# Up stage issued in written order, ten groups computed ahead, fewer score steps a load

## Chip, cores, metric

The kernel runs on one core of a Trainium2 chip. The metric is the device time of one execution in microseconds (us); smaller is better. All data are float32. A product is made from two parts of each operand, a rounded high part and the rest (hi and lo), as three matmuls: hi by hi, hi by lo, lo by hi.

## Reference, cut to what matters

One layer of a decoder on 1024 tokens of width 1024:

```
h = rmsnorm(x);  z = h @ w_in                      # seven blocks of 512 columns
mix_a = gated linear recurrence of four blocks     # chunks, decays, states
mix_b = gate_b * causal_conv3(gate_c * conv_h)
x = x + rmsnorm(concat(mix_a, mix_b) @ w_out)
h = rmsnorm(x);  u = causal_conv3(h @ ffn_w_up)    # 1024 -> 2 x 2816
gate, val = split(u)
x = x + rmsnorm((silu(gate) * val) @ ffn_w_down)   # 2816 -> 1024
```

## The kernel before, in words

The instructions are written in Python; a list scheduler then orders each engine's instructions by its own cost model, with the place in the program as priority. Each engine runs its list in order. `high_priority` lifts what stands in it.

**Mixers.** The 1024 tokens are two halves of 512. For each half come projections of 512 columns (f, q, i, g: `gemm_quad`, eight k tiles of 128 rows, loaded and split two at a time) and twelve convolution tiles (`gemm_tile`, three for each of four column blocks, in `z_conv`). Small steps of the recurrence wait in a queue, `fill`. `tick` pops one between blocks of matmuls. The score steps come first: products and diagonals, then fourteen "levels" (seven widths by two groups of heads). A level is eight short matmuls `sl` (L358), then on DVE a predicated copy (L359) and three multiplications (L364, L366, L368), on whose result the next level's matmuls wait. Chunk steps follow. `rate` says how many ticks a load of two k tiles gets (L206). `z_conv` pops a number per tile from `rates`.

**Front.** The first weights of f come in two halves (`pieces=2`, L130), cast on DVE (L132, L133). x comes transposed, tile by tile (L229); ACT scales its hi part (L232), DVE makes its lo part (L233). A small chain (L594 to L599) makes the bound of the forget gate.

**Up stage.** The product by `w_up` and its convolution run in 22 groups (`order`: gate column block j and so on), each a 2x2 Strassen-Winograd scheme with seven products, P1 to P7, of 12 matmuls of 512 columns. A group has two PSUM banks `pG` (g) and two `pV` (v):

- `head_weights` loads the group's 1 MB of weights w (L729) and splits two of the four blocks (h_x, l_x). `head_1` is P1 into g[1], copied to g[0] by ACT (L753); `head_2` is P2 onto g[0].
- `mid_weights` makes three sums on DVE (L774 to L776) and splits them into h_t (ACT) and l_t (DVE). These tiles exist once, so group n's h_t can only be written when P7 of group n-1 has read the old ones.
- `mid` is P6 onto g[1], a copy s2 of it by ACT (L741), P5 into v[1], v[0] = v[1] + s2 on DVE (L791), P7 onto g[1], a copy s3, and v[1] += s3 on DVE (L794).
- `tail_weights` splits the last two blocks (h_b, l_b). P4 (onto g[1]) and P3 (onto v[0]) use them, in the next group's turn of the loop.
- `gate` is a convolution of g (ACT L803, DVE L804, L805) and a Silu (L817). `value` is the same of v, then the product with the gate (L824) and, after each second group, four sums for the down stage (L832 to L835).

In the trace the weights' names tell the products: c2 is P6, c1 P5, c7 P7, c4 P4, c3 P3, uhi and ulo P1 and P2.

**Groups ahead.** P1 and P2 need only the first token half. For the groups in `AHEAD` they are computed before the loop, in pairs (`ahead`, matmuls `pA`), between the output projection and the loop, and stored; `take_back` loads them and ACT copies them into g (L768). Such a group is "short": in the loop it has P3 and P4 of the group before and its own P6, P5, P7. A long group has P1, P4, P2, P3, P6, P5, P7. `AHEAD` holds eight groups: 0, 1, 3, 5, 7, 9, 11, 13. `marked` (L737) is a matmul that only sets a bank's state. While the `pA` run, ACT and DVE build the right operands of P3 to P7 (comb, L858 to L879).

The down stage follows: seven products, with 44 k tiles of gated values read back.

Of the kernel before, what the change touches and what calls it, by code (L numbers as in the profile page):

```python
# [2 lines left out]

# [1 line left out]

# [36 lines left out]
def decoder_kernel(ctx: ExitStack, tc: tile.TileContext, x, xT, w_sq, w_cv, w_out, w_up, w_dn,  # L42
# [68 lines left out]
    def split(src, hi, lo):  # L111
        nc.scalar.copy(hi, src)  # L112
        nc.vector.tensor_tensor(lo, src, hi.bitcast(F32), ALU.subtract)  # L113

    def load_w(src, shape, name, pieces=1, queue=None, gains=None):

        raw = wp.tile(list(shape), F32, tag="wraw", bufs=3, name=f"r_{name}")
        hi = wp.tile(list(shape), F32R, tag="whi", name=f"h_{name}")
        lo = wp.tile(list(shape), F32R, tag="wlo", name=f"l_{name}")
        if gains is not None:  # L120
            nc.sync.dma_start(raw[:], src)
            for i, g in enumerate(gains):
                nc.scalar.mul(hi[:, i], raw[:, i], g)
                nc.vector.scalar_tensor_tensor(
                    lo[:, i], raw[:, i], g, hi[:, i].bitcast(F32), ALU.mult, ALU.subtract)
            return hi, lo
        n = shape[1] // pieces
        for i in range(pieces):
            s = slice(i * n, (i + 1) * n)
            (queue or nc.sync).dma_start(raw[:, s], src[:, s])  # L130
            if queue is not None:
                nc.vector.tensor_copy(hi[:, s], raw[:, s])  # L132
                nc.vector.tensor_tensor(lo[:, s], raw[:, s], hi[:, s].bitcast(F32), ALU.subtract)  # L133
            else:
                split(raw[:, s], hi[:, s], lo[:, s])
        return hi, lo
# [28 lines left out]
    def mm3_fm(ps, whi, wlo, ahi, alo, first, last, more=False):  # L165
        nc.tensor.matmul(ps, whi, ahi, start=first, stop=False, skip_group_check=more)  # L166
        nc.tensor.matmul(ps, whi, alo, start=False, stop=False, skip_group_check=more)  # L167
        nc.tensor.matmul(ps, wlo, ahi, start=False, stop=last, skip_group_check=more)  # L168

    def mm3_tm(ps, ahi, alo, whi, wlo, first, last, more=False):  # L170
        nc.tensor.matmul(ps, ahi, whi, start=first, stop=False, skip_group_check=more)  # L171
        nc.tensor.matmul(ps, ahi, wlo, start=False, stop=False, skip_group_check=more)  # L172
        nc.tensor.matmul(ps, alo, whi, start=False, stop=last, skip_group_check=more)  # L173

    def gemm_tile(src, act, name):

# [6 lines left out]
    def gemm_quad(src, act, name, token_major, groups, order=None, pieces=1, rate=1, hooks=None, queue=None,  # L183
                  gains=None, banks=None):

        order = order or list(range(len(act)))
        pss = [banks(f"p_{name}_{j}") if banks else ps_mm.tile([P, TH], F32, tag="mm", name=f"p_{name}_{j}")
               for j in range(4)]
        ws, i0 = {}, 0
        for gi, n in enumerate(groups):  # L190
            ks = range(i0, i0 + n)
            for i in ks:
                if i // 2 not in ws:
                    ws[i // 2] = load_w(src[order[i] // 2], (P, 2, TH), f"{name}_{i // 2}", pieces,
                                         queue if i == 0 else None, (gains or {}).get(order[i] // 2))
            for j in range(4):
                for i in ks:
                    whi, wlo = (w[:, i % 2, :] for w in ws[i // 2])
                    js = slice(j * P, (j + 1) * P)
                    ahi, alo = act[order[i]]  # L200
                    first, last = i == 0, i == len(act) - 1
                    if token_major:
                        mm3_tm(pss[j][:], ahi[:, js], alo[:, js], whi, wlo, first, last)
                    else:
                        mm3_fm(pss[j][:], whi[:, js], wlo[:, js], ahi, alo, first, last)
                if (i0 + n) % 2 == 0 and j % (4 // rate) == 4 // rate - 1:  # L206
                    tick()
            i0 += n
            if hooks and gi in hooks:
                hooks[gi]()  # L210
        return pss
# [13 lines left out]
    def make_h(hf):  # L225
        act = []
        for k in range(KD):
# [2 lines left out]
            hi, lo = hslot(f"hi{hf}_{k}"), hslot(f"lo{hf}_{k}")  # L230
            g = vcol(V_PRE + k)
            nc.scalar.mul(hi[:], xk[:], g)  # L232
            nc.vector.scalar_tensor_tensor(lo[:], xk[:], g, hi[:].bitcast(F32), ALU.mult, ALU.subtract)  # L233
            act.append((hi[:], lo[:]))
            if hf == 0:
                yield act
# [337 lines left out]


    hgen = make_h(0)
    act_a = next(hgen)

    class Lazy:


        def __len__(self):
            return KD

        def __getitem__(self, k):
            while len(act_a) <= k:
                next(hgen)
            return act_a[k]


    lbt = zp.tile([P, 4, H], F32, name="lbt")
    lbp = vec[:, V_LB : V_LB + H]
    e_, s_, lb, oml = (lbt[:, i, :] for i in range(4))
    nc.vector.tensor_tensor(e_, lbp, lbp, ALU.subtract)  # L594
    nc.scalar.activation(e_, e_, AF.Exp)
    nc.vector.reciprocal(s_, e_)
    nc.vector.tensor_tensor(s_, s_, e_, ALU.mult)
    nc.vector.tensor_tensor(lb, s_, s_, ALU.subtract)
    nc.vector.tensor_scalar(oml, lb, -1.0, 1.0, ALU.mult, ALU.add)  # L599

    first = {}

    def scale_a():
        for _ in hgen:
            pass
        nc.sync.dma_start(ident[:], ident_d)
        with tc.high_priority():
            pc = aux("pc", (P, NC_H + P))
            for c in range(NC_H):
                nc.tensor.matmul(pc[:, c : c + 1], sums[0][:, c * C : (c + 1) * C], ones[:, 0:1], start=True, stop=True)  # L610
            first["r"] = rstd(pc[:, :NC_H], D, "x0")
            first["rows"] = by_token(0, first["r"], pc[:NC_H, NC_H:])

    def scale_a_rows():
        nc.scalar.activation(warm[:], first["r"][:, 0:1], AF.Sigmoid)
        first["FU"] = evac_f(0, pss, first["rows"])

    pss = gemm_quad(w_sq[0], Lazy(), "f0", False, (1, 1, 1, 1, 1, 1, 1, 1), pieces=2, queue=nc.sync,
                    hooks={6: scale_a})
    r0 = first["r"]  # L620
    qss = gemm_quad(w_sq[1], act_a, "q0", False, PAIRS, hooks={0: scale_a_rows}, banks=aux)
# [12 lines left out]
    def mixers(hf, act, F, UW, rb, rq, r, ma, conv_rates, at_end=None):  # L634
        fill.extend(score_steps(hf, F, UW))
        v = evac_v(hf, gemm_quad(w_sq[2], act, f"i{hf}", True, PAIRS, rate=2), rq)
        gg = evac_g(hf, gemm_quad(w_sq[3], act, f"g{hf}", True, PAIRS, rate=2), r)
        fill.extend(chunk_steps(hf, F, UW, v, gg, ma))
        mb = z_conv(hf, act, rb, conv_rates, at_end)
        return [(ma[0][:, j, :], ma[1][:, j, :]) for j in range(H)] + mb  # L640
# [1 line left out]
    def ma_tiles(hf):  # L642
# [1 line left out]

    act_b = []
    later = []
    mix_a = mixers(0, act_a, F0, UW0, rb0, rq0, r0, ma_tiles(0), (1, 1, 1, 1, 1, 1, 1, 1, 1, 1, 2, 2),
                   at_end=(lambda: later.append(stats(1)), lambda: act_b.extend(list(make_h(1))[-1])))
    r1 = later[0]

# [7 lines left out]
    gain = post_gain(0, ap)  # L658
    x1a = out_proj(0, mix_a, gain)
    evac_q(1, gemm_quad(w_sq[1], act_b, "q1", False, PAIRS, rate=2), rb1, UW1)  # L660
    mix_b = mixers(1, act_b, F1, UW1, rb1, rq1, r1, ma_tiles(1), (1, 1, 1, 1, 1, 1, 1, 1, 2, 2, 2, 2))
    a1 = []
    x1b = out_proj(1, mix_b, gain, hooks={0: lambda: make_a1(x1a, a1), 1: lambda: tick(len(fill))})

# [11 lines left out]
    take(1, [a1[k][0] for k in range(KH)], [a1[k][1] for k in range(KH)])  # L676
    take(2, [a1[k + KH][0] for k in range(KH)], [a1[k + KH][1] for k in range(KH)])

    def product(ps, w, i, op, first=False):
        hi, lo = w  # L680
        for k in range(KH):
            mm3_fm(ps, hi[:, i, k], lo[:, i, k], a_hi[op][k], a_lo[op][k], first and k == 0, k == KH - 1, not first)

    order = [j + s * NG for j in range(NG) for s in range(2)]
    box = [{} for _ in order]
    AHEAD = (0, 1, 3, 5, 7, 9, 11, 13)
    nc.vector.tensor_scalar(neg[:], vec[:, V_PREF : V_PREF + KH], -1.0, None, ALU.mult)


    ah_w = zh.tile([P, 2, 2, KH, P], F32, tag="F", name="ah_w")
# [3 lines left out]
    def ahead(ns, keep):  # L696
# [4 lines left out]
        to = [keep.get(n, ah_f[:, i]) for i, n in enumerate(ns)]  # L701
        for p, op in ((1, 1), (0, 2)):
            for i, n in enumerate(ns):
                product(banks[i][:], (ah_x[:, i, 0], ah_x[:, i, 1]), p, op, p == 1)
                nc.scalar.copy(to[i][:, p], banks[i][:])
                if p == 0 and n not in keep:
                    nc.sync.dma_start(f_d[n], to[i])

    for i in (1, 3, 5):
        ahead(AHEAD[i : i + 2], {})  # L710
    tick(len(fill))
    scope1.close()
# [5 lines left out]
    def ft(tag, shape, name, bufs=1, dt=F32, pool=None):  # L718
        return (pool or fp).tile(list(shape), dt, tag=tag, bufs=bufs, name=name)

    def parts(src, tags, shape, name, bufs=1, pool=None):
        hi = ft(tags[0], shape, f"h{name}", bufs, F32R, pool)
        lo = ft(tags[1], shape, f"l{name}", bufs, F32R, pool)
        split(src, hi[:], lo[:])
        return hi, lo

    def load_up(n):
# [7 lines left out]
    def marked(ps):  # L735

        nc.tensor.matmul(ps, a_hi[1][0][:, :P], a_hi[1][0], start=True, stop=True)  # L737

    def snap(ps, name):
        t = ft("s", (P, TH), name, 4, pool=pa[0])  # L740
        nc.scalar.copy(t[:], ps)  # L741
        return t

    def head_weights(n):
        b = box[n]
        w = b["w"] = load_up(n)
        b["x"] = parts(w[:, 0:2], ("xh", "xl"), (P, 2, KH, P), f"_x{n}", 2, pb[0])

    def head_1(n):
        b = box[n]  # L750
# [8 lines left out]
    def take_back(n):  # L759
# [5 lines left out]
        if n < 2:  # L765
            marked(g[:, 0])
            marked(g[:, 1])
        nc.scalar.copy(g[:], t[:])  # L768

    def mid_weights(n):  # L770
        b = box[n]
# [7 lines left out]
    def mid(n):  # L779
# [8 lines left out]
            product(v[:, 1], b["t"], 1, 5, True)  # L788
        if n < 2:
            marked(v[:, 0])  # L790
        nc.vector.tensor_tensor(v[:, 0], v[:, 1], s2[:], ALU.add)  # L791
        product(a, b["t"], 2, 7)
        s3 = snap(a, f"s3_{n}")
        nc.vector.tensor_tensor(v[:, 1], v[:, 1], s3[:], ALU.add)  # L794

    def tail_weights(n):
        b = box[n]
# [20 lines left out]

    def value(n):
        b = box[n]  # L820
        v = ft("av", (P, T), f"v{n}", 2, pool=pa[0])
        conv(b.pop("v"), v, NF + order[n])
        g = b["o"]
# [325 lines left out]
```

## Time and profile before

| | us |
|---|---|
| median of 3 runs | 1128.95 |
| the profiled execution | 1128.56 |
| its span (first to last instruction) | 1126.7 |
| busy: PE, weight loads, DVE, ACT | 1103.9, 910.6, 839.1, 511.2 |

| stretch, us | stage |
|---|---|
| 0 to 430 | mixers of both halves, first output projection |
| 430 to 517 | second output projection, groups ahead |
| 517 to 907 | up stage |
| 907 to 1127 | down stage, last rows |

PE is the matmul engine, PEld its weight load, DVE the vector engine, ACT the scalar engine, SP the engine that issues most DMAs. Matmuls are pipelined: one of 512 columns is shown as 0.39 us long, but the next starts 0.227 us after it. So time is lost where starts lie further apart. A row of the timeline gives start, length, engine, line, operation, output and inputs, count, and in brackets the idle time before and what ended it.

### The profile page before, as it was taken

What the parts mean: (1) busy time and instruction counts of PE and PEld (TensorE: products, weight loads), DVE (VectorE), ACT (ScalarE), POOL (GpSimd) and SP (SyncE); (2) the same over time, 40 slices, a digit from 0 to 9 for tenths busy, and PEclk for the clock granted to TensorE, in tenths of its full rate; (3) what the DMA queues carried; (4) which work ended last, traced back from release to release, by engine and by line L of the source; (5) the groups of instructions that cost most, each with busy time, mean ns of one, the idle gap of its engine ahead of it and who ended that gap; (6) DMA issues with size and microseconds to landing.
All of it is one profiled execution on the core that took longest, in us unless ns stands there. A gap on an engine that the chain in (4) does not pass through costs nothing.

```text
span 1126.7 us, 13472 instructions
## 1 busy us (share of the span) xinstructions
PE 1103.9 (98%) x5090; PEld 910.6 (81%) x5090; DVE 839.1 (74%) x1199; ACT 511.2 (45%) x755; POOL 10.0 (1%) x18
## 2 busy tenths in 40 slices
PE   9999999999999999999999999999999999999997
PEld 7878888888878888877787777878888888888885
DVE  7578677537687777387989888887878866865787
ACT  6444254435433337366443544444444534445541
POOL 1100000000000000000000000000000000000000
PEclk9999999999999999999999999999999999999999
DMA  8522224325312237174323434233222369867633
GB/s 289 208 65 71 94 77 132 119 94 187 113 57 94 83 109 259 64 253 169 112 103 140 159 122 154 76 126 140 103 85 93 122 215 410 336 225 251 200 109 121
DMA packets 55088, 167.23 MB, mean 148 GB/s; under 512 B 5480, under 2 KB 5744, under 8 KB 52080
## 3 DMA queue, kind: packets, MB, share of 16 engines
q1 hardware_dynamic: 54704, 165.76, 42.1%
q8 instruction: 40, 0.66, 0.3%
q0 software_dynamic: 160, 0.52, 0.1%
q14 instruction: 24, 0.20, 0.1%
q10 hardware_dynamic: 160, 0.09, 0.0%
HBM read 132.01 MB, written 34.34 MB: 148 GB/s over the span
## 4 chain that ended last, share of the span: by engine, by line
PE 88%; DVE 5%; ACT 4%; DMA 2%; issue 1%; DVEq 0%; SPq 0%; ACTq 0%
PE pG L166 7%; PE pG L167 7%; PE pG L168 7%; PE pV L166 3%; PE pV L168 3%; PE pV L167 3%; PE pX L171 3%; PE pX L173 3%; PE pX L172 3%; PE pY L171 2%; PE pY L172 2%; PE pY L173 2%; PE sl L358 2%; PE p_wo L173 2%; PE p_wo L171 2%; PE p_wo L172 2%
## 5 line engine op out<-in xcount | busy, mean ns | idle before, releaser
L113 DVE TENSOR_TENSOR ls<-s,hs 128x1024 fp32r<-128x1024 f32 (+1 forms) x40 | 45.2, 1129 | 44.9 <-ACT hs L112 44.9
L112 ACT CAST hs<-s 128x1024 fp32r<-128x1024 f32 (+1 forms) x40 | 39.1, 977 | 73.4 <-PE pY L172 31.2
L172 PE MATMUL pY<-lw,hs 128*128 128x512 f32 x132 | 51.3, 389 | 0.0
L173 PE MATMUL pY<-hw,ls 128*128 128x512 f32 x132 | 51.3, 389 | 0.0
L171 PE MATMUL pY<-hw,hs 128*128 128x512 f32 x132 | 51.2, 389 | 0.0
L817 ACT ACTIVATE g<-g 128x1024 f32<-128x1024 f32 x22 | 23.4, 1062 | 59.2 <-DVE g L805 59.2
L112 ACT CAST h_t<-t 128x1536 fp32r<-128x1536 f32 x22 | 32.6, 1481 | 38.5 <-PE pG L167 35.8
L113 DVE TENSOR_TENSOR l_t<-t,h_t 128x1536 fp32r<-128x1536 f32 x22 | 38.6, 1756 | 9.6 <-ACT h_t L112 9.6
L171 PE MATMUL pX<-hw,hs 128*128 128x512 f32 x116 | 45.1, 389 | 0.0
L172 PE MATMUL pX<-lw,hs 128*128 128x512 f32 x116 | 45.1, 389 | 0.0
L173 PE MATMUL pX<-hw,ls 128*128 128x512 f32 x116 | 45.1, 389 | 0.0
L166 PE MATMUL pG<-uhi,h_x 128*128 128x512 f32 x112 | 44.4, 396 | 0.0
L167 PE MATMUL pG<-ulo,h_x 128*128 128x512 f32 x112 | 44.3, 395 | 0.0
L168 PE MATMUL pG<-uhi,l_x 128*128 128x512 f32 x112 | 44.1, 394 | 0.0
L166 PE MATMUL pG<-c2h,h_t 128*128 128x512 f32 x88 | 34.9, 396 | 8.0 <-ACT h_t L112 6.7
L804 DVE SCALAR_TENSOR_TENSOR v<-pV,vec,v 128x1023 f32<-128x1023 f32 x22 | 28.2, 1280 | 18.0 <-ACT v L803 17.9
L113 DVE TENSOR_TENSOR l_b<-w,h_b 128x1024 fp32r<-128x1024 f32 x22 | 26.8, 1220 | 17.3 <-ACT h_b L112 17.3
L803 ACT ACTIVATE g<-pG,vec 128x1024 f32<-128x1024 f32 x22 | 24.5, 1115 | 28.7 <-PE pG L168 28.6
L803 ACT ACTIVATE v<-pV,vec 128x1024 f32<-128x1024 f32 x22 | 24.5, 1112 | 26.6 <-PE pV L168 26.5
L359 DVE COPY_PREDICATED S<-m_lev,sl 128x512 f32<-128x512 uint8 x28 | 24.9, 891 | 14.8 <-PE sl L358 14.8
L345 ACT COPY lhs<-UW 128x512 f32<-128x512 f32 x28 | 18.5, 662 | 37.3 <-DVE UW L366 37.3
L166 PE MATMUL pG<-c4h,h_b 128*128 128x512 f32 x88 | 34.8, 395 | 0.7 <-ACT s L741 0.7
(339 smaller groups left out, 3416.5 us busy)
## 6 DMA issues: line engine op xcount, KB each, us to landing
w<-w_up SPq DMA_DIRECT2D x22, 1024.0 KB, 4.8
b<-w_dn SPq DMA_DIRECT2D x35, 512.0 KB, 8.6
s<-s_d SPq DMA_DIRECT2D x33, 512.0 KB, 4.7
s_d<-g SPq DMA_DIRECT2D x22, 512.0 KB, 3.3
s_d<-S SPq DMA_DIRECT2D x11, 768.0 KB, 3.9
r_wo<-w_out SPq DMA_DIRECT2D x16, 512.0 KB, 3.5
xT<-xT SPq DMA_DIRECT2D x16, 256.0 KB, 3.8
r_q<-w_sq SPq DMA_DIRECT2D x8, 512.0 KB, 3.8
```

The source lines that it names most:

```text
L112: nc.scalar.copy(hi, src)
L113: nc.vector.tensor_tensor(lo, src, hi.bitcast(F32), ALU.subtract)
L166: nc.tensor.matmul(ps, whi, ahi, start=first, stop=False, skip_group_check=more)
L167: nc.tensor.matmul(ps, whi, alo, start=False, stop=False, skip_group_check=more)
L168: nc.tensor.matmul(ps, wlo, ahi, start=False, stop=last, skip_group_check=more)
L171: nc.tensor.matmul(ps, ahi, whi, start=first, stop=False, skip_group_check=more)
L172: nc.tensor.matmul(ps, ahi, wlo, start=False, stop=False, skip_group_check=more)
L173: nc.tensor.matmul(ps, alo, whi, start=False, stop=last, skip_group_check=more)
L359: nc.vector.copy_predicated(view(S, 2 * X, o + h, (X - h, 2), (2 * h, n), (1, h)), m_lev[:, li].rearrange("p x g (b h) -> p x (g b) h", h= ...
L803: nc.scalar.mul(a[:], c, wc[2])
L804: nc.vector.scalar_tensor_tensor(a[:, 1:], c[:, : T - 1], wc[1], a[:, 1:], ALU.mult, ALU.add)
L817: nc.scalar.activation(g[:], g[:], AF.Silu)
```

## The change

- `product` puts an edge from the last product to the next (`issue_after`), so the loop's products go out on PE as written; those of `ahead` are free.
- In `value`, v[1] += s3 now stands behind P3; v[0] = v[1] + s2 gets high priority.
- `AHEAD` has ten groups at even places: 0, 2, ..., 18.
- ACT's split of h_x is issued behind the s3 copy two groups before; ACT's copy in `take_back` is kept in program order.
- The g projection has (2, 1, 2, 1) ticks a load in place of 2 each; the convolution tiles get two more, spread over the list.
- In the front, the first weights are issued ahead of x, their second half by ACT; DVE's lo part of x is issued behind the first weight cast; the chain of the gate's bound moves to the end of the first projection.

```diff
-            (queue or nc.sync).dma_start(raw[:, s], src[:, s])
+            (queue[i] if queue else nc.sync).dma_start(raw[:, s], src[:, s])
             if queue is not None:
-                nc.vector.tensor_copy(hi[:, s], raw[:, s])
+                front.append(nc.vector.tensor_copy(hi[:, s], raw[:, s]))
...
+                r = rate[i0 // 2] if isinstance(rate, tuple) else rate
+                if (i0 + n) % 2 == 0 and j % (4 // r) == 4 // r - 1:
                     tick()
...
-            nc.vector.scalar_tensor_tensor(lo[:], xk[:], g, hi[:].bitcast(F32), ALU.mult, ALU.subtract)
+            with tc.issue_after(front[0].ins):
+                nc.vector.scalar_tensor_tensor(lo[:], xk[:], g, hi[:].bitcast(F32), ALU.mult, ALU.subtract)
...
-    nc.vector.tensor_tensor(e_, lbp, lbp, ALU.subtract)
+    def lower_bound():
+        tc.keep_in_program_order(nc.vector.tensor_tensor(e_, lbp, lbp, ALU.subtract))
...
         nc.sync.dma_start(ident[:], ident_d)
+        lower_bound()
...
-        gg = evac_g(hf, gemm_quad(w_sq[3], act, f"g{hf}", True, PAIRS, rate=2), r)
+        gg = evac_g(hf, gemm_quad(w_sq[3], act, f"g{hf}", True, PAIRS, rate=(2, 1, 2, 1)), r)
...
-    mix_a = mixers(0, act_a, F0, UW0, rb0, rq0, r0, ma_tiles(0), (1, 1, 1, 1, 1, 1, 1, 1, 1, 1, 2, 2),
+    mix_a = mixers(0, act_a, F0, UW0, rb0, rq0, r0, ma_tiles(0), (2, 1, 1, 2, 1, 1, 2, 1, 1, 2, 1, 1),
...
-    mix_b = mixers(1, act_b, F1, UW1, rb1, rq1, r1, ma_tiles(1), (1, 1, 1, 1, 1, 1, 1, 1, 2, 2, 2, 2))
+    mix_b = mixers(1, act_b, F1, UW1, rb1, rq1, r1, ma_tiles(1), (2, 1, 2, 1, 2, 1, 2, 1, 2, 1, 2, 1))
...
+    line = []
-    def product(ps, w, i, op, first=False):
+    def product(ps, w, i, op, first=False, in_line=True):
         hi, lo = w
-        for k in range(KH):
-            mm3_fm(ps, hi[:, i, k], lo[:, i, k], a_hi[op][k], a_lo[op][k], first and k == 0, k == KH - 1, not first)
+        with tc.issue_after(line[-1]) if in_line and line else nullcontext():
+            for k in range(KH):
+                mm = mm3_fm(ps, hi[:, i, k], lo[:, i, k], a_hi[op][k], a_lo[op][k], first and k == 0, k == KH - 1,
+                            not first)
+        if in_line:
+            line.append(mm.ins)
...
-    AHEAD = (0, 1, 3, 5, 7, 9, 11, 13)
+    AHEAD = (0, 2, 4, 6, 8, 10, 12, 14, 16, 18)
...
-    for i in (1, 3, 5):
+    for i in range(1, len(AHEAD) - 1, 2):
         ahead(AHEAD[i : i + 2], {})
...
-        b["x"] = parts(w[:, 0:2], ("xh", "xl"), (P, 2, KH, P), f"_x{n}", 2, pb[0])
+        b["x"] = parts(w[:, 0:2], ("xh", "xl"), (P, 2, KH, P), f"_x{n}", 2, pb[0], snaps[2 * n - 3] if n > 1 else None)
...
-        nc.scalar.copy(g[:], t[:])
+        tc.keep_in_program_order(nc.scalar.copy(g[:], t[:]))
...
-        nc.vector.tensor_tensor(v[:, 0], v[:, 1], s2[:], ALU.add)
+        with tc.high_priority():
+            nc.vector.tensor_tensor(v[:, 0], v[:, 1], s2[:], ALU.add)
         product(a, b["t"], 2, 7)
-        s3 = snap(a, f"s3_{n}")
-        nc.vector.tensor_tensor(v[:, 1], v[:, 1], s3[:], ALU.add)
+        b["s3"] = snap(a, f"s3_{n}")
...
     def value(n):
         b = box[n]
+        c22 = b["v"][:, 1]
+        nc.vector.tensor_tensor(c22, c22, b.pop("s3")[:], ALU.add)
```

## Rows read from the trace of the kernel before

**Rows 1.** The page: busy time by engine, share of the span, instructions.

```profile
PE 1103.9 (98%) x5090; PEld 910.6 (81%) x5090; DVE 839.1 (74%) x1199; ACT 511.2 (45%) x755; POOL 10.0 (1%) x18
```

**Rows 2.** PE's waits over the span: total us, times, longest us.

```profile
PE pG L166 <- ACT h_t L112: 6.7, 5, 1.3
PE sl L358 <- DVE UW L366: 2.8, 7, 0.5
...
PE pG L166 <- DVE S L835: 1.3, 1, 1.3
PE pG L166 <- ACT s L741: 0.7, 1, 0.7
```

**Rows 3.** Windows: us, PE, PEld, DVE, ACT, POOL busy (count), clock, DMA, GB/s.

```profile
666.34:700.85 34.51, 33.18 (x144) 26.97 (x144) 29.56 (x31) 16.73 (x19) 0.00 (x0) 1.00 0.36 134
...
806.92:845.46 38.54, 38.54 (x170) 31.57 (x169) 30.71 (x31) 16.80 (x20) 0.00 (x0) 1.00 0.28 102
...
468.66:517.48 48.82, 48.62 (x225) 39.21 (x224) 42.45 (x75) 34.56 (x64) 0.00 (x0) 1.00 0.56 203
```

**Rows 4.** Timeline of PE where short group 9 begins.

```profile
664.62 0.39 PE L168 MATMUL pG<-c7h,l_t 128*128 128x512 f32 x1
666.34 0.50 PE L166 MATMUL pG<-c2h,h_t 128*128 128x512 f32 x1 [1.34 <-DVE S L835]
...
667.14 0.40 PE L166 MATMUL pG<-c4h,h_b 128*128 128x512 f32 x1
```

**Rows 5.** Timelines of ACT and DVE around the same place.

```profile
656.15 1.01 ACT L768 COPY pG<-f 128x1024 f32<-128x1024 f32 x1
...
664.82 1.47 ACT L112 CAST h_t<-t 128x1536 fp32r<-128x1536 f32 x1 [4.62 <-PE pG L167]
666.19 0.58 ACT L741 COPY s<-pG 128x512 f32<-128x512 f32 x1
...
663.01 0.69 DVE L791 TENSOR_TENSOR pV<-pV,s 128x512 f32<-128x512 f32 x1
...
666.32 1.76 DVE L113 TENSOR_TENSOR l_t<-t,h_t 128x1536 fp32r<-128x1536 f32 x1
...
673.28 1.28 DVE L804 SCALAR_TENSOR_TENSOR v<-pV,vec,v 128x1023 f32<-128x1023 f32 x1 [0.88 <-ACT v L803]
```

**Rows 6.** Start of the up stage: PE, SP's weight loads, and their landing (page).

```profile
527.00 0.39 PE L168 MATMUL pG<-c7h,l_t 128*128 128x512 f32 x1
528.07 0.50 PE L166 MATMUL pG<-c4h,h_b 128*128 128x512 f32 x1 [0.68 <-ACT s L741]
...
521.39 1.37 SPq L729 DMA_DIRECT2D w<-w_up  x2
...
w<-w_up SPq DMA_DIRECT2D x22, 1024.0 KB, 4.8
```

**Rows 7.** Score levels of the second half: PE and DVE; one of the first half.

```profile
318.34 1.14 PE L358 MATMUL sl<-UW,lhs 128*128 128x128 f32 x8 [0.44 <-DVE UW L366]
...
317.50 0.69 DVE L366 TENSOR_TENSOR UW<-UW,F 128x512 f32<-128x512 f32 x1
...
116.78 0.73 DVE L359 COPY_PREDICATED S<-m_lev,sl 128x512 f32<-128x512 uint8 x1
```

**Rows 8.** Timeline of the front: SP, ACT, DVE and PE.

```profile
0.73 0.39 SPq L229 DMA_DIRECT2D xT<-xT  x1
1.19 0.89 SPq L130 DMA_DIRECT2D r_f<-w_sq  x2
...
4.78 0.71 ACT L232 ACTIVATE hi<-xT,vec 128x512 fp32r<-128x512 f32 x1
...
5.60 0.75 DVE L233 SCALAR_TENSOR_TENSOR lo<-xT,vec,hi 128x512 fp32r<-128x512 f32 x1
6.27 0.76 DVE L132 CAST h_f<-r_f 128x512 fp32r<-128x512 f32 x2
...
6.83 0.47 PE L166 MATMUL p_f<-hi,h_f 128*128 128x512 f32 x1 [1.57 <-DVE h_f L132]
```

More of the change, by code (lines that the diff above doesn't have):

```diff
@@ L1 @@
 from collections import deque
-from contextlib import ExitStack
+from contextlib import ExitStack, nullcontext
 import numpy as np
@@ L113, in split @@
         nc.vector.tensor_tensor(lo, src, hi.bitcast(F32), ALU.subtract)
+    front = []
     def load_w(src, shape, name, pieces=1, queue=None, gains=None):
@@ L167, in mm3_fm @@
         nc.tensor.matmul(ps, whi, alo, start=False, stop=False, skip_group_check=more)
-        nc.tensor.matmul(ps, wlo, ahi, start=False, stop=last, skip_group_check=more)
+        return nc.tensor.matmul(ps, wlo, ahi, start=False, stop=last, skip_group_check=more)
     def mm3_tm(ps, ahi, alo, whi, wlo, first, last, more=False):
@@ L172, in mm3_tm @@
         nc.tensor.matmul(ps, ahi, wlo, start=False, stop=False, skip_group_check=more)
-        nc.tensor.matmul(ps, alo, whi, start=False, stop=last, skip_group_check=more)
+        return nc.tensor.matmul(ps, alo, whi, start=False, stop=last, skip_group_check=more)
     def gemm_tile(src, act, name):
@@ L205, in gemm_quad @@
                         mm3_fm(pss[j][:], whi[:, js], wlo[:, js], ahi, alo, first, last)
-                if (i0 + n) % 2 == 0 and j % (4 // rate) == 4 // rate - 1:
+                r = rate[i0 // 2] if isinstance(rate, tuple) else rate
+                if (i0 + n) % 2 == 0 and j % (4 // r) == 4 // r - 1:
                     tick()
@@ L576, in decoder_kernel @@
     hgen = make_h(0)
-    act_a = next(hgen)
     class Lazy:
+        made = ()
         def __len__(self):
@@ L585, in __getitem__ @@
         def __getitem__(self, k):
-            while len(act_a) <= k:
-                next(hgen)
-            return act_a[k]
+            while len(self.made) <= k:
+                self.made = next(hgen)
+            return self.made[k]
     lbt = zp.tile([P, 4, H], F32, name="lbt")
@@ L593, in decoder_kernel @@
     e_, s_, lb, oml = (lbt[:, i, :] for i in range(4))
-    nc.vector.tensor_tensor(e_, lbp, lbp, ALU.subtract)
[L595 to L599, printed above, removed]
+    def lower_bound():
+        tc.keep_in_program_order(nc.vector.tensor_tensor(e_, lbp, lbp, ALU.subtract))
+        nc.scalar.activation(e_, e_, AF.Exp)
+        nc.vector.reciprocal(s_, e_)
+        nc.vector.tensor_tensor(s_, s_, e_, ALU.mult)
+        nc.vector.tensor_tensor(lb, s_, s_, ALU.subtract)
+        nc.vector.tensor_scalar(oml, lb, -1.0, 1.0, ALU.mult, ALU.add)
     first = {}
@@ L616, in scale_a_rows @@
         first["FU"] = evac_f(0, pss, first["rows"])
-    pss = gemm_quad(w_sq[0], Lazy(), "f0", False, (1, 1, 1, 1, 1, 1, 1, 1), pieces=2, queue=nc.sync,
+    act_a = Lazy()
+    pss = gemm_quad(w_sq[0], act_a, "f0", False, (1, 1, 1, 1, 1, 1, 1, 1), pieces=2, queue=(nc.sync, nc.scalar),
                     hooks={6: scale_a})
@@ L677, in decoder_kernel @@
     take(2, [a1[k + KH][0] for k in range(KH)], [a1[k + KH][1] for k in range(KH)])
-    def product(ps, w, i, op, first=False):
+    line = []
+    def product(ps, w, i, op, first=False, in_line=True):
         hi, lo = w
-        for k in range(KH):
-            mm3_fm(ps, hi[:, i, k], lo[:, i, k], a_hi[op][k], a_lo[op][k], first and k == 0, k == KH - 1, not first)
+        with tc.issue_after(line[-1]) if in_line and line else nullcontext():
[4 more added lines that the diff above has]
+            line.append(mm.ins)
     order = [j + s * NG for j in range(NG) for s in range(2)]
     box = [{} for _ in order]
-    AHEAD = (0, 1, 3, 5, 7, 9, 11, 13)
-    nc.vector.tensor_scalar(neg[:], vec[:, V_PREF : V_PREF + KH], -1.0, None, ALU.mult)
+    AHEAD = (0, 2, 4, 6, 8, 10, 12, 14, 16, 18)
+    tc.keep_in_program_order(
+        nc.vector.tensor_scalar(neg[:], vec[:, V_PREF : V_PREF + KH], -1.0, None, ALU.mult))
     ah_w = zh.tile([P, 2, 2, KH, P], F32, tag="F", name="ah_w")
@@ L703, in ahead @@
             for i, n in enumerate(ns):
-                product(banks[i][:], (ah_x[:, i, 0], ah_x[:, i, 1]), p, op, p == 1)
+                product(banks[i][:], (ah_x[:, i, 0], ah_x[:, i, 1]), p, op, p == 1, False)
                 nc.scalar.copy(to[i][:, p], banks[i][:])
@@ L719, in ft, with parts @@
         return (pool or fp).tile(list(shape), dt, tag=tag, bufs=bufs, name=name)
-    def parts(src, tags, shape, name, bufs=1, pool=None):
+    def parts(src, tags, shape, name, bufs=1, pool=None, behind=None):
         hi = ft(tags[0], shape, f"h{name}", bufs, F32R, pool)
         lo = ft(tags[1], shape, f"l{name}", bufs, F32R, pool)
-        split(src, hi[:], lo[:])
+        with tc.issue_after(behind) if behind else nullcontext():
+            nc.scalar.copy(hi[:], src)
+        nc.vector.tensor_tensor(lo[:], src, hi[:].bitcast(F32), ALU.subtract)
         return hi, lo
@@ L737, in marked @@
         nc.tensor.matmul(ps, a_hi[1][0][:, :P], a_hi[1][0], start=True, stop=True)
+    snaps = []
     def snap(ps, name):
         t = ft("s", (P, TH), name, 4, pool=pa[0])
-        nc.scalar.copy(t[:], ps)
+        snaps.append(nc.scalar.copy(t[:], ps).ins)
         return t
```

## The prediction

> **What bounds the kernel now.** First the page's busy times: PE is busy 98% of the span [rows 1], which leaves at most 22.8 us for any change that takes no matmul away. The list of PE's waits is next: the largest by far is PE waiting for ACT's h_t in the up stage, 6.7 us in 5 waits, and a sixth of the same length is put down to DVE's L835 [rows 2]; after it come 2.8 us in 7 waits of the score levels. Third, the windows by pair of groups. A pair of long groups takes 38.54 us with PE busy throughout, 2.75 us for each of its 14 products. A pair of one long and one short group has 12 products, 33.0 us at that pace, and takes 34.51 [rows 3]. Last the timeline at a short group's start: P7 of the group before ends, two matmuls of P6 come next and wait 1.34 us, and P4, whose operands were long there, stands behind them [rows 4]. ACT begins h_t at 664.82, within P7's last matmul, because the tile exists once; PE goes on as it ends [rows 5]. The place in the order costs the time, not the amount of ACT's or DVE's work: ACT had idled 4.62 us before that cast.
>
> **The change part by part.**
>
> *Written order.* In a short group P3 and P4 now come before P6: 24 matmuls, 5.5 us, in which h_t (1.47) and l_t (1.76) can be made [rows 5]. One wait costs 1.72 us between starts less 0.227, and 0.11 more for the first matmul after it (0.50 in place of 0.39) [rows 4]: 1.60 us. Six of them: -9.6 us. What is late next is the s3 copy of 0.58, which P4 needs and P3 covers with 2.75 us, and v[0] = v[1] + s2, which P3 needs: DVE started it at 663.01 and took 0.69 [rows 5], so it was done 1.3 us before P7 ended, and it now has priority.
>
> *Group 1 becomes long.* At 528.07 P4 of group 0 waited for s3: 1.07 us between starts less 0.227, plus 0.11: 0.95 us [rows 6]. P1 of group 1 now lies between them: -0.95. P1 needs its 1 MB of weights, issued at 521.39 and 4.8 us on the way [rows 6], then h_x and l_x, some 2.3 us by the nearest casts (h_t and l_t, of half as many columns again, take 3.2 [rows 5]): 528.5, a microsecond too late as things stand. But the start of the loop moves back by a whole pair ahead, 10.9 us of PE, with at most 5 us more for ACT (four copies of 0.58 and two casts shorter than 1.47 [rows 5]), so the load goes out earlier; I take 0, with +1.2 as the other end. Two marking matmuls fall away, 0.45 us, but they filled PE's wait for s2 before P7 of group 0: together 0.
>
> *Two more groups ahead.* Their P1 and P2 move from the loop to the stretch before it, PE's time unchanged. That stretch is dense now: 48.62 of 48.82 us [rows 3]. One more boundary between pairs, at the price of the three there are (0.2 us idle together): 0 to 0.4, I take +0.2. The added DMAs (half a megabyte of weights, a store and a load for each group) find queues busy 0.56 before the loop and 0.36 in it [rows 3]; without that cover they would delay a copy that is needed some 5 us after its group's turn begins. SP carries them in line with the weight loads.
>
> *The s3 addition behind P3.* The same 0.69 us of DVE, now ahead of ACT's value pass; off PE's path as long as the two v banks suffice. 0.
>
> *Ten short groups instead of six that mattered.* Each pair must fit 29.56 us of DVE into 33.0 [rows 3], 90%, where the long pairs run at 80% without a wait. The cost of that is what the trace does not show: nothing at one end; at the other 1.5 us a pair, which would be today's 34.5. The short windows today wait for order and not for DVE, so I take the value near the lower end, 0.1 us a pair: +1.0.
>
> *Front.* PE starts at 6.83, when DVE's weight cast is done; the cast began at 6.27, behind the lo part of x (0.75 from 5.60) [rows 8]. With the weights issued 0.46 earlier and cast first, PE can start when ACT's hi part is there: 4.78 + 0.71, and the x transfer one issue slot (0.46) later: about 6.0. Its second matmul then needs the lo part, 0.75 more. So 0.5 gained, between 0 and 0.9. The chain of the gate's bound is about a microsecond of tiny instructions on DVE, hidden beside the q projection, and would cost that microsecond if it were not. One page speaks against more from ACT's queue: the Trainium skill, DMA: Bandwidth & Descriptors, section "Issuing engines are not separate DMA queues", says that all issuing engines share the same transfer engines and only issue time is saved. By it the sum stays; with a stream of its own for the second half it would be 0.4 us less. No row here tells the two apart.
>
> *Score steps.* A wait costs its idle time plus the 0.16 between a matmul's modelled end and the next start: 0.60 at 318.34 [rows 7]. In the second half three levels of the g projection wait; with four ticks at 24 matmuls' distance instead of 12, two of these should go, and one that did not wait may start to. -0.7, between -1.1 and 0. In the first half the waits are in the first ticks, which keep their places: 0. The two displaced steps meet the convolution tiles.
>
> **The sum.** 1128.56 - 9.6 - 0.95 + 0.2 + 1.0 - 0.5 - 0.7 = 1118.0 for the profiled execution; the median stands 0.4 above it, so 1118.4 for the median, 0.9% less. A difference under about 0.5% can't be told from none here.
>
> **Rivals.**
>
> *ACT's order keeps P6 waiting.* The copy from `take_back` (1.01) is kept in program order, which puts it behind s3 and ahead of h_t: 0.58 + 1.01 + 1.47 + 1.76 = 4.8 us after P7 [rows 5], some 5.2 with handovers, against 5.5 and 0.45 until l_t is first read. If DVE begins a value pass (1.28) or the s3 addition (0.69) just before l_t, that is 6.5 to 7.2, and P6 waits 0.5 to 1.2 us in ten groups: 1123.5 to 1130, I say 1125. The Trainium skill, TensorE: Matmul & The Clock Gate, section "Architectural detail", calls the queues of ACT and DVE strictly first in, first out; by that rule such a wait is not mended at run time. The trace agrees: at 656.15 the copy stood between two passes [rows 5] and nothing overtook it. For it: the slack is only 0.7 us. Against: the scheduler knows of l_t's reader. Chance 0.15.
>
> *DVE becomes the bound (slower).* Today's long and short pair leaves DVE 4.95 us idle (34.51 - 29.56), mostly until ACT passes arrive. The new pair has 3.5. If the idle time stays at 4.95, all ten pairs stay at 34.5: +14 us on the sum, 1132. If also one s3 addition a pair falls into the chain before the value pass, 35.2: 1139. It decides from idle time over 4.7 us a pair, where the gain of about 10.6 is gone. Against it: DVE idles with nothing waiting behind, and the long pairs idle 7.8 us without harm. Chance 0.13: 0.07 beyond 0.5% slower, 0.06 short of it.
>
> *Doubled score steps wait.* Two ticks at one place put a level right behind the one it depends on, across three DVE operations of about 0.7 us (0.73, 0.69 [rows 7]). If no matmul is put between, 2.1 us each, for about four such levels: 1126.8. Against it: the scheduler moved levels behind some matmuls before. Chance 0.05.
>
> *The order does not hold* and the six waits stay would give 1127; the edges name the matmuls, so I give this 0.02.
>
> **How the numbers follow.** The forecast and what lies within 3 us of it get 0.65. Faster by over 0.5% (below 1123.3): 0.65 and 0.07 of the first rival, 0.72. Slower by over 0.5%: 0.07. The rest, 0.21, lies between. The range goes from all favourable ends together (1115) to the upper part of the first rival, the third and the fourth: 1128. Left out are the second rival and the worst of the first, under 0.2.
>
> **What would show it.** In PE's waits the h_t row should vanish. Short pairs should take 33.0 to 33.4 us, with P3 and P4 ahead of P6, and DVE busy 90% in them. The first p_f matmul should start near 6.0, the second group's P1 without a wait for w. Wrong would be new PE waits at a short group's P6 (first rival), at P3 for L791 or P1 for PSUM (second), or before `sl` in the convolution tiles (third).

## The result and the profile after

The changed kernel takes 1119.18 us (median of 5, 1118.46 to 1123.76) where the kernel before takes 1128.94: a ratio of 0.991, with a 95% interval of 0.9884 to 0.9937. The profiled execution took 1119.18 us at a span of 1117.4; before it was 1128.56 at 1126.7. The forecast was 1118.4. The time came out as foretold. The waits that the prediction wanted to remove are the ones that went; the experiments show that another part of the change removes them than the one it gave the credit to.

The page of the changed kernel, busy times, against [rows 1]:

```profile
PE 1101.6 (99%) x5088; PEld 910.6 (81%) x5088; DVE 831.5 (74%) x1199; ACT 514.8 (46%) x759; POOL 10.8 (1%) x18
```

PE has lost 2.3 us of busy time and the span 9.3: most of what went is waiting. PE's waits over the span, total us, times, longest us, against [rows 2]:

```profile
PE sl L362 <- DVE UW L370: 2.4, 6, 0.5
PE mt L455 <- DVE mx L432: 1.6, 1, 1.6
...
PE p_f L168 <- ACT hi L235: 0.9, 1, 0.9
PE pG L168 <- ACT s L762: 0.5, 1, 0.5
```

The h_t row, its sixth wait under DVE's name and the 0.7 us for s3 are gone. The row for s that stands there now is another wait: P7 of group 0 for s2, where two marking matmuls lay before. The row for mt (a small product behind mx, the last step of a score chunk) is new among the large ones: it was 0.4 us before. Two stretches of the changed kernel, a pair with a short group and the stretch of the ahead pairs (columns as in [rows 3]):

```profile
657.44:690.31 32.87, 32.87 (x146) 27.05 (x145) 28.66 (x29) 15.85 (x18) 0.00 (x0) 1.00 0.38 137
...
469.14:529.59 60.45, 60.01 (x274) 48.24 (x273) 49.19 (x84) 39.94 (x71) 0.00 (x0) 1.00 0.58 205
```

A pair takes 32.87 us with PE busy throughout, where it took 34.51. The short group in the timeline of PE, against [rows 4]:

```profile
657.21 0.39 PE L170 MATMUL pG<-c7h,l_t 128*128 128x512 f32 x1
657.44 0.39 PE L168 MATMUL pV<-c3h,h_b 128*128 128x512 f32 x1
...
660.16 0.39 PE L168 MATMUL pG<-c4h,h_b 128*128 128x512 f32 x1
...
662.88 0.39 PE L168 MATMUL pG<-c2h,h_t 128*128 128x512 f32 x1
```

P7 (c7), P3 (c3), P4 (c4), P6 (c2) follow each other without a pause. ACT and DVE at the same place, against [rows 5]:

```profile
651.23 1.02 ACT L789 COPY pG<-f 128x1024 f32<-128x1024 f32 x1
...
657.41 1.48 ACT L742 CAST h_t<-t 128x1536 fp32r<-128x1536 f32 x1 [4.62 <-PE pG L169]
658.80 0.58 ACT L762 COPY s<-pG 128x512 f32<-128x512 f32 x1
...
658.93 1.76 DVE L743 TENSOR_TENSOR l_t<-t,h_t 128x1536 fp32r<-128x1536 f32 x1 [2.98 <-ACT h_t L742]
660.60 0.69 DVE L843 TENSOR_TENSOR pV<-pV,s 128x512 f32<-128x512 f32 x1
```

h_t and l_t are made between 657.41 and 660.69, 2.2 us before P6 starts. The s3 addition (L843) runs at 660.60, while P4 is on, and PE doesn't notice it. The copy of `take_back` was done at 652.25, ahead of P7, and no P6 waits, so the prediction's first rival didn't come about.

By stretches, taking the times of the same matmul in both traces, and 48 matmuls of 0.2275 us (10.9 us) as moved out of the loop:

| stretch | foretold | profile |
|---|---|---|
| before the ahead pairs (front, score steps) | -1.2 | +0.5 |
| ahead pairs, without the moved matmuls | +0.2 | +0.7 |
| up stage, with the moved matmuls put back | -9.55 | -11.3 |
| after it | 0 | +0.7 |

The last row wasn't followed; in the other traces it lies between +0.1 and +0.6, and higher in the two with extra DVE passes.

### The profile page after: what moved, and what is told of

Read it like the earlier page. It is cut to its first block, busy times and chain, and to the rows that moved or that the text cites. A ratio compares the mean times of both kernels' runs of the same rounds, so it can differ in the third digit from the quotient of the medians.

```text
span 1117.4 us, 13477 instructions
## 1 busy us (share of the span) xinstructions
PE 1101.6 (99%) x5088; PEld 910.6 (81%) x5088; DVE 831.5 (74%) x1199; ACT 514.8 (46%) x759; POOL 10.8 (1%) x18
## 4 chain that ended last, share of the span: by engine, by line
PE 90%; DVE 4%; DMA 2%; ACT 2%; issue 2%; SPq 0%; DVEq 0%; ACTq 0%
PE pG L168 7%; PE pG L170 7%; PE pG L169 7%; PE pV L168 4%; PE pV L170 4%; PE pV L169 4%; PE pX L174 3%; PE pX L175 3%; PE pX L173 3%; PE pY L174 3%; PE pY L173 3%; PE pY L175 3%; PE sl L362 2%; PE p_wo L175 2%; PE p_wo L173 2%; PE p_wo L174 2%
## 5 line engine op out<-in xcount | busy, mean ns | idle before, releaser
L168 PE MATMUL pG<-uhi,h_x 128*128 128x512 f32 x96 | 38.0, 396 | 0.0
L169 PE MATMUL pG<-ulo,h_x 128*128 128x512 f32 x96 | 38.0, 395 | 0.0
L170 PE MATMUL pG<-uhi,l_x 128*128 128x512 f32 x96 | 37.8, 394 | 0.0
L825 DVE SCALAR_TENSOR_TENSOR g<-pG,vec,g 128x1023 f32<-128x1023 f32 x22 | 28.1, 1279 | 9.2 <-ACT g L824 9.2
L168 PE MATMUL pG<-c7h,h_t 128*128 128x512 f32 x88 | 34.4, 391 | 0.5 <-ACT s L762 0.5
L762 ACT COPY s<-pG 128x512 f32<-128x512 f32 x44 | 25.7, 584 | 19.9 <-PE pG L170 19.9
L168 PE MATMUL pV<-c3h,h_b 128*128 128x512 f32 x88 | 34.5, 392 | 0.0
```

The source lines that it names most:

```text
L170: return nc.tensor.matmul(ps, wlo, ahi, start=False, stop=last, skip_group_check=more)
L762: snaps.append(nc.scalar.copy(t[:], ps).ins)
L825: nc.vector.scalar_tensor_tensor(a[:, 1:], c[:, : T - 1], wc[1], a[:, 1:], ALU.mult, ALU.add)
```

## The experiments

Twelve runs followed, eleven of them with an edit. Loop times below go from the first pV matmul to the 30th of pX.

**The ordering edges taken out.** The changed kernel with this edit:

```
-        with tc.issue_after(line[-1]) if in_line and line else nullcontext():
+        with nullcontext():
```

> The changed kernel without the ordering edges between the products; everything else stays, the s3 addition behind P3 too. Theory A (the prediction's): the edges bring P3 and P4 ahead of P6, so without them the ten short groups wait for h_t again, 1.6 us each: 1119.2 + 16 = 1135. Theory B (the place of the s3 addition decides): P3 writes the same PSUM tile as that addition, so with the addition behind P3 nothing holds P3 back and the scheduler puts it first by itself; the edges add nothing: 1119 to 1120.5, no h_t row in PE's waits.

Measured: 1118.46 us, ratio 0.9895 (0.9881 to 0.991), the same as with the edges within the intervals. The first of PE's waits in this kernel:

```profile
PE sl L362 <- DVE UW L370: 2.4, 6, 0.5
PE mt L455 <- DVE mx L432: 1.4, 1, 1.4
```

No h_t row came back among the rest. In all nine short groups that follow another group, P3 and P4 still stand ahead of P6. Theory A falls: with the s3 addition behind P3 the edges do nothing.

**The s3 addition put back.** The changed kernel, edges and all:

```
         product(a, b["t"], 2, 7)
-        b["s3"] = snap(a, f"s3_{n}")
+        s3 = snap(a, f"s3_{n}")
+        nc.vector.tensor_tensor(v[:, 1], v[:, 1], s3[:], ALU.add)
...
-        c22 = b["v"][:, 1]
-        nc.vector.tensor_tensor(c22, c22, b.pop("s3")[:], ALU.add)
```

> The changed kernel with the s3 addition back in its old place, ahead of P3; the ordering edges stay. Theory A: that addition was priced at nothing, so 1119.2 within 1. Theory B: P3 stands first by the edges and now waits for ACT's h_t cast (1.48), the s3 copy (0.58) and DVE's addition (0.69), some 2.9 us with handovers in each of the ten short groups: 1119.2 + 29 = 1148, with a new row of PE at P3 waiting for DVE's addition.

Measured: 1174.83 us, ratio 1.0394 (1.0378 to 1.0409), 3.9% slower than the kernel before. The wait that theory B foretold, in nine groups:

```profile
PE pV L168 <- DVE pV L816: 33.6, 9, 3.7
```

One of them in the timelines of PE, ACT and DVE, and the window behind it:

```profile
680.20 0.79 PE L168 MATMUL pV<-c3h,h_b 128*128 128x512 f32 x1 [3.74 <-DVE pV L816]
...
676.27 1.47 ACT L742 CAST h_t<-t 128x1536 fp32r<-128x1536 f32 x1 [4.62 <-PE pG L169]
677.65 0.58 ACT L762 COPY s<-pG 128x512 f32<-128x512 f32 x1
...
677.78 1.76 DVE L743 TENSOR_TENSOR l_t<-t,h_t 128x1536 fp32r<-128x1536 f32 x1 [2.88 <-ACT h_t L742]
679.45 0.69 DVE L816 TENSOR_TENSOR pV<-pV,s 128x512 f32<-128x512 f32 x1
```

```profile
680.20:685.30 5.10, 5.10 (x12) 4.04 (x13) 3.59 (x4) 0.00 (x0) 0.00 (x0) 0.50 0.00 0
```

P3 waits until the addition (L816) is done, and starts right behind it. It reads nothing of it: P3 writes `v[:, 0]`, the addition `v[:, 1]`. What they share is the tile pV, so by the code it is the tile that ties them; a kernel with a tile for each half was not tried. The edges put P3 first, so PE stands: h_t, l_t and the addition one after the other make 3.74 us of idle time, not 2.9, because DVE has l_t ahead of the addition. Then comes a price that no theory had: in the window behind this wait the granted clock is 0.50 (1.2 of 2.4 GHz), and P3's 12 matmuls come every 0.43 us instead of every 0.23, some 2.4 us more. Behind the nine waits 6 to 14 matmuls run at that pace. The loop is 54.8 us longer than in the changed kernel: 33.6 of waiting, the rest mostly that.

**The s3 addition moved, and nothing else.** The kernel before with the reverse of that diff.

> The kernel before with one edit: the s3 addition moved behind P3. No edges, eight groups ahead at the old places. Theory A: the six waits for h_t stay, 1128.9 within 1. Theory B: they go with this edit alone, and the wait for s3 in the first short group too: 1128.9 - 9.6 - 0.9 = 1118.4, within 1.5.

Measured: 1119.92 us, ratio 0.9907 (0.9893 to 0.9922): within the intervals the whole gain of the change. The loop went from 397.85 to 387.35 us: -10.50, where the prediction's two terms for the waits make -10.55. (This profiled execution began with p_f matmuls at half the pace, as the last section tells; that cost it some 1.5 us ahead of the loop.) The h_t and s3 rows are gone from PE's list; its largest is `sl`, 2.8 us in 7, as before.

**The edges, and nothing else.** The kernel before, with `product` ending in a `line` as in the change.

> The kernel before with one edit: the ordering edges between the products. The s3 addition stays ahead of P3. Theory A: the six waits go, 1128.9 - 9.6 - 0.9 = 1118.4. Theory B: P3 takes the place of P6 as the one that waits, some 2.9 us in each of seven short groups in place of 1.6: 1128.9 - 10.5 + 20 = 1138.5, slower than the kernel before.

Measured: 1156.33 us, ratio 1.0231 (1.0214 to 1.0248), with one new row:

```profile
PE pV L166 <- DVE pV L800: 23.0, 7, 3.7
```

Theory B again, and dearer than its 1138.5, for the same two reasons: the waits reach 3.74 us, and behind the five longest the matmuls come every 0.43 us again. These four settle it: the place of the addition decides in both directions; the edges do nothing with it moved and harm without.

**DVE loaded with more work.** The changed kernel with one, then two, extra passes per group; they add a number into a tile that nobody reads any more:

```
         nc.vector.tensor_tensor(g[:], g[:], v[:], ALU.mult)
+        for _ in range(1):
+            nc.vector.tensor_tensor(v[:], g[:], v[:], ALU.add)
```

> The changed kernel with one more DVE pass of 1.23 us at the end of each group's value step, into a tile that nobody reads afterwards: 2.46 us a pair, DVE some 32.0 of the 32.9 us of a pair with a short group. Theory (DVE's idle time in a pair is free to use; the prediction's second rival put its need too high): no new wait, 1119 to 1122. Rival (DVE needs about 3.3 us of idle time a pair for its hand-overs with ACT): 2.4 us a pair, ten pairs, 1143.

> The same with two such passes: 4.92 us a pair, DVE 34.5 us of work in a pair that takes PE 32.9. Theory: DVE is the bound of the ten short pairs now, 34.5 and a little more: 1.6 to 2.5 us a pair, 1135 to 1144. Rival (3.3 us of idle time stay needed): 37.8 a pair, 1168.

Measured: 1120.48 us (ratio 0.9915, 0.9899 to 0.9931) with one, 1121.96 us (0.9926, 0.9911 to 0.9941) with two. The loop took 375.67 us without, 375.67 with one and 377.46 with two. A pair with a short group in the kernel with one pass:

```profile
658.46:691.33 32.87, 32.87 (x145) 27.05 (x144) 30.92 (x32) 15.85 (x18) 0.00 (x0) 1.00 0.37 136
```

The same pair and the next in the kernel with two:

```profile
657.22:690.09 32.87, 32.87 (x146) 27.06 (x145) 32.16 (x34) 15.86 (x17) 0.00 (x0) 1.00 0.40 144
...
690.09:723.29 33.20, 33.12 (x146) 26.94 (x145) 32.75 (x35) 15.78 (x17) 0.00 (x0) 1.00 0.36 132
```

One pass in each group adds 2.26 us to the 28.66 of a pair, 1.13 for each pass of 1.22, because passes that follow each other without a gap overlap by some 0.09. DVE then idles 1.95 us a pair, and PE doesn't wait. With two passes DVE has 28.66 + 4 x 1.13 = 33.18 us of work a pair, more than PE's 32.87. The first four pairs still take 32.87, while DVE falls behind; the five after them take 33.2 to 33.3, because P1 of their long groups now waits for DVE's l_x. PE and DVE at the first such place:

```profile
704.40 0.50 PE L170 MATMUL pG<-uhi,l_x 128*128 128x512 f32 x1
...
703.13 1.22 DVE L743 TENSOR_TENSOR l_x<-w,h_x 128x1024 fp32r<-128x1024 f32 x1
```

So with two passes DVE does become the bound, as that expectation's theory had it, and at 0.34 us a pair instead of 1.6 to 2.5: it counted more work for DVE than there is, and the wait begins only where the work itself is longer than the pair. In both kernels the first pX matmuls then wait 0.7 us for their weights.

**The last chunk's mx ahead of the ahead pair's splits.** The wait for mt in the changed kernel, timelines of DVE, ACT and PE:

```profile
437.00 0.15 DVE L156 SCALAR_TENSOR_TENSOR rs_o<-rt_o,rs_o 128x4 f32<-128x4 f32 x1
438.96 1.23 DVE L113 TENSOR_TENSOR ah_x<-ah_w,ah_x 128x1024 fp32r<-128x1024 f32 x1 [1.80 <-ACT ah_x L112]
...
437.88 1.05 ACT L112 CAST ah_x<-ah_w 128x1024 fp32r<-128x1024 f32 x1 [2.05 <-DMA ah_w<-w_up]
...
440.88 1.12 DVE L432 SCALAR_TENSOR_TENSOR mx<-o,rs_o,gg 128x128 f32<-128x128 f32 x4
...
441.38 0.30 PE L455 MATMUL mt<-ident,mx 128*128 128x128 f32 x1 [1.61 <-DVE mx L432]
```

In the middle of the rstd chain DVE stands 1.80 us for ACT's cast, and ACT 2.05 us for the weights to land, although the rest of the chain (the run below shows it) could go on. The edit, on the changed kernel:

```
+                    op = nc.vector.scalar_tensor_tensor(
                         mx[:, js], po[:, js], r[:, j : j + 1], gg[c][:, js], ALU.mult, ALU.mult)
+                mxs.append(op.ins)
...
-            split(ah_w[:, i], ah_x[:, i, 0], ah_x[:, i, 1])
+            with tc.issue_after(mxs[-1]):
+                split(ah_w[:, i], ah_x[:, i, 0], ah_x[:, i, 1])
```

> The changed kernel with the lo splits of the first ahead pair held on DVE behind the last score chunk's mx. Theory (the place of the splits between that chunk's rstd chain and its mx makes the 1.6 us wait of PE at mt, and swallows what front and score steps gained): rstd ends near 436.7, mx near 437.9, before PE asks for mt at 439.8; the mt row vanishes, pA starts 1.6 earlier, 1119.2 - 1.6 = 1117.6. Rival (something else, ACT's mah or the next weights, is late there too): the mt row moves to another tile and less than 0.5 us comes through, 1118.9.

Measured: 1116.93 us, ratio 0.9885 (0.9869 to 0.9902). DVE and PE in its trace:

```profile
436.57 0.16 DVE L156 SCALAR_TENSOR_TENSOR rs_o<-rt_o,rs_o 128x4 f32<-128x4 f32 x1
436.77 1.13 DVE L433 SCALAR_TENSOR_TENSOR mx<-o,rs_o,gg 128x128 f32<-128x128 f32 x4
...
437.38 0.27 PE L457 MATMUL mt<-ident,mx 128*128 128x128 f32 x1
```

The wait is gone, and between the 240th p_wo matmul and the first pA 1.8 us are won. The cause of the wait is shown.

**The column sums later.** The same, with pc (L618) held on PE behind the 72nd p_f matmul, its order edge naming that matmul.

> As the run before, and the column sums of x (pc) held on PE behind the 72nd matmul of p_f instead of the 62nd. Theory (the front's 0.6 us was given back because pc came before DVE's acc was done): p_q starts 0.5 earlier than in the run before, and 1117.6 - 0.5 = 1117.1. Rival (the row scales, now about 1.8 us later, make the score levels or p_i wait by as much as is saved): 1117.6 or up to 1 us more, with longer sl rows.

Measured: 1119.15 us, ratio 0.9901 (0.9886 to 0.9916). From the 62nd p_f matmul to the first of p_q it lost 1.1 us against the run before: the transposes behind pc now wait 1.0 us for DVE's rs_x. The rival's direction, at another place: the chain from pc through rstd to those transposes has no slack there. Its profiled execution also began with p_f matmuls at half the pace (see the last section) and came to that 62nd matmul 1.4 us later, so the 2.2 us between the two medians need not all be the edit's.

**Only the two edits that showed something.** The kernel before with the s3 addition moved and mx first; and the changed kernel as it is, on the same chip.

> The kernel before with two edits alone: the s3 addition behind P3, and the lo splits of the first ahead pair behind the last mx. None of the rest of the change. Theory (with the wait at mt gone, the front's and the score steps' gains of the rest come through, some 1 to 1.5 us): 1118.0 to 1118.5, so 1 to 1.5 us above the run with mx first on the changed kernel. Rival (the rest of the change brings nothing at all): 1117 within 0.5, as that run.

> The changed kernel as it is, on the same chip as the three runs before, so that they can be set against it: 1119.2 within 0.7, 2 us above the runs with mx first.

Measured: 1117.55 us (ratio 0.989, 0.9875 to 0.9905) and 1118.10 us (0.9892, 0.9878 to 0.9905). The first comes out as its rival had it; the second lies below what was expected. What the change has beside the s3 addition can't be told from nothing in these times, whose intervals are some 3 us wide.

**mx first without the edges, and with more warming.**

> The changed kernel with mx first and without the ordering edges. Theory (the edges do nothing in the ten short groups, as in the run without them alone): 1116.5 to 1117. Rival (with the ahead pairs starting earlier the scheduler mixes other products and waits come back): above 1118, with a new PE row in the up stage.

> The changed kernel with mx first, and 11 warming matmuls in place of 9, so that PE is busy until the first p_f. In some profiled runs the first 12 matmuls of p_f came every 0.43 us instead of every 0.23, 1.3 us lost, in others not, and PE had idled 0.9 to 1.5 us before them. Theory (that idle stretch lets the clock fall): every run has the fast front, 1116.5 with a spread under 0.5. Rival (the slow front has another cause, or the two matmuls only stand in front of p_f): no change in the spread, 1117 to 1117.5.

Measured: 1117.71 us (ratio 0.9888, 0.9871 to 0.9904) without the edges, 1117.85 us (0.9891, 0.9877 to 0.9906) with `WARM = 11`. No new wait in the up stage in the former, whose time lies between its theory and its rival. In the latter the idle time ahead of p_f fell to 0.32 us, pc then waited 0.9 us for rs_x, and the runs still spread over 1.8 us; its theory isn't borne out. On this chip all three kernels with mx first lie 0.25 to 0.55 us below the changed kernel, less than the intervals: the stretch from the 240th p_wo matmul to the first pA is 1.8 us or more shorter than in the changed kernel in each of their traces, and the times don't show it yet.

## Why the prediction was right, and where it was not

*Written order, -9.6, and group 1 long, -0.95.* The size was right, and so was what the new order does: P3 and P4 cover h_t and l_t. What brings that order about was wrong: it was put down to the edges, and for group 0 to group 1's being long. The prediction listed what P3 and P4 would need once they came first, the s3 copy and v[0], and left out what P3 waits for without reading it: the s3 addition in the other half of its tile. With that addition moved, the scheduler puts P3 first by itself. In the trace of before it stood ahead of P3's first matmul:

```profile
668.00 0.69 DVE L794 TENSOR_TENSOR pV<-pV,s 128x512 f32<-128x512 f32 x1
...
669.21 0.39 PE L166 MATMUL pV<-c3h,h_b 128*128 128x512 f32 x1
```

These rows were there to be read. So the edges alone give 1156 us, and the addition's move alone gives -10.50 of loop. That the two marking matmuls and the wait that they filled come to nothing together was right: 0.45 went, and between the starts at P7 of group 0 0.45 came.

*The s3 addition, 0.* This is the step that failed. It was priced at 0, as 0.69 us of DVE that stay off PE's path. Its place is worth the two terms above: -10.50 us of loop by itself. That the total came out right all the same is luck in this respect: the change happened to hold the one edit that its largest term needs. The misses by stretch, +1.7, +0.5, -1.7 and +0.7 in the table, cancel in part too.

*Ten short groups, +1.0.* 0: nine pairs take 32.87 us each. The up stage with the moved matmuls put back is 0.76 shorter than with the s3 edit alone; that wasn't followed.

*One more boundary, +0.2.* In this profile +0.7; in most of the other traces with ten groups the stretch takes 60.02 us, which is +0.28. Right.

*Front, -0.5.* The first p_f matmul came 0.63 earlier, at 6.20, and the 62nd 0.60. But pc stands behind it, and waits 0.24 us for DVE's acc, which is done no sooner: at the first p_q matmul 0.07 are left. In the second profiled execution of the changed kernel pc doesn't wait, and 0.27 are left. The rule of the Trainium skill, DMA: Bandwidth & Descriptors, section "Issuing engines are not separate DMA queues", that was weighed here would have shown in 0.4 us; no run tells its two sides apart.

*Score steps, -0.7.* One of the three waits of the second half went, where two were to go. From the end of that half's f projection to the start of its out projection it is -0.50, and all of it was given back at mt, where PE came 0.77 earlier and waited 1.61 in place of 0.39, because the landing of a DMA sets when mx is done. Both small gains were real where they were made. The prediction didn't ask which wait behind them was set by something other than PE.

*The rivals.* ACT's order: the copy stands ahead of s2, not behind s3. The prediction let the copy at 656.15 speak for the rule of the Trainium skill, TensorE: Matmul & The Clock Gate, section "Architectural detail", that the queues of ACT and DVE are strictly first in, first out. That row can't, since nothing is seen to have been ready behind the copy. The DVE rows of the changed kernel at 437.00 to 440.88 agree with it: steps of the rstd chain that were ready stand behind a split that waits 1.80 us. DVE as the bound: the idle time it was said to need was 4.7 us a pair; 1.95 cost nothing, and the wait comes only when DVE's work exceeds the pair. Doubled score steps: they didn't wait. That the order would not hold was given 0.02; it holds, and does so without the edges. No rival said that another part of the change makes the gain, nor that the edges alone would cost 26 us.

## What to carry to other kernels

A wait can hang on a tile and not on data: ask for each instruction that is to come earlier who wrote last to the tile that it touches, in any half, and move that writer behind it before the order is forced. An order that the scheduler refuses to choose has a reason; take the reason away, and it may choose that order by itself, as here, whereas forcing it cost 2.3%. A gain ahead of a wait that a DMA or another engine's chain sets goes into that wait.

## What the runs showed of the hardware

In the two kernels with the edges and the s3 addition in its old place P3 waits 3.74 us 14 times. Behind each of them 6 to 14 matmuls ran at 0.43 us from start to start, in 11 cases from the first one on, in three after two that came near the full pace; the window shown above has a granted clock of 0.50. After waits of 1.41 and 2.94 us in the kernel with the edges alone the 12 matmuls of P3 started within 2.64 and 2.62 us, near full pace. Reckoned against a start every 0.2275 us, the wait of 2.94 us cost 3.2 us, and those of 3.74 us cost 5.4 to 6.9.

The start of the kernel shows the same two paces. In 6 of the 14 profiled executions the first 7 to 9 p_f matmuls came every 0.43 us or more, and the 15th began 4.75 to 5.22 us after the first; in 7 it began 3.28 to 3.31 us after it, and in the one with more warming 3.65. PE had idled 0.99 to 1.53 us ahead of p_f in those 6 and 0.32 to 1.65 in the others, so the length of that idle time alone doesn't decide it. Nor does the code: of the four kernels with the old front two began at half pace, of the nine executions with the new front and no added warming four. (The expectation of the run with more warming says 12 slow matmuls; it was 7 to 9.) The kernel with mx first and without the edges, PE's timeline and a window:

```profile
6.29 2.07 PE L168 MATMUL p_f<-hi,h_f 128*128 128x512 f32 x4 [1.03 <-ACT hi L235]
8.16 0.63 PE L169 MATMUL p_f<-lo,h_f 128*128 128x512 f32 x1
8.59 0.63 PE L170 MATMUL p_f<-hi,l_f 128*128 128x512 f32 x1
```

```profile
7.30:8.30 1.00, 1.00 (x4) 0.80 (x3) 0.97 (x3) 0.58 (x2) 0.00 (x0) 1.00 1.06 406
```

The granted clock of that window reads 1.00, although the pace is that of 0.50 elsewhere; at the start of the span the column doesn't show the pace. The Trainium skill, TensorE: Matmul & The Clock Gate, section "What's actually happening", says that the number of slow matmuls at a kernel's start differs from run to run. These traces agree as far as they go, with none to 9 matmuls at half pace under the same front; both of the changed kernel's own profiled executions began at the full pace. A start at half pace puts the 15th p_f matmul 1.4 to 1.9 us later, more than any of the small terms of the prediction, so that they could be seen in traces and not in times.
